# Differential attention heads: the inverse slope goes into q, the score correction products use 128 rows with zeros, and the DMA scratch is 8 KB

## The chip, the cores and the metric

The kernel runs on one core of one Trainium2 chip. The metric is the time of one execution on the device in microseconds (us), as the median of several runs. Five engines work side by side, each through its own list of instructions in order: TensorE (PE; its weight loads are shown as PEld), VectorE (DVE), ScalarE (ACT), GpSimd (POOL) and SyncE (SP), which issues most of the loads from memory. POOL issues transfers too.

## The reference

The model is an encoder of two layers over 512 tokens of 1024 features. Each layer modulates its input, projects it, runs two kinds of attention side by side (eight heads with latent projections, "MLA", and eight differential heads), gates and adds their outputs, and adds the residual; then comes a feed-forward block (layer 0) or a mixture of eight experts with two per token (layer 1). What the change touches are the differential heads. Cut to that:

```python
slopes = 2.0 ** (-8.0 * jnp.arange(1, 9) / 8)          # 1/2, 1/4, ... 1/256
# q, k: [token, head, 2 halves, 64]; v: [token, head, 128]
sc = einsum('bqhmd,bkhmd->mbhqk', q, k) * 64 ** -0.5
sc = sc - slopes[h] * abs(pos_q - pos_k)
p = softmax(sc, axis=-1)
a = p[0] - lam * p[1]
o = einsum('bhqk,bkhd->bqhd', a, v)                    # then an RMS norm per head
```

A head has two halves of 64 features, each with scores and a softmax of its own; the slope of the distance halves from head to head.

## The kernel before, in words

All matrix products are made in a reduced float32 type (float32r). To keep float32 accuracy each operand is split into a larger part and a remainder, and three products are added: large by large, large by remainder and remainder by large (`mm3`, lines 127 to 129). For weights, `wsplit` does this: ACT copies the loaded tile to the larger part `wh` (L111), and DVE subtracts to get `wl` (L113). In the attention part this subtraction is done by POOL instead (`W["eng"] = G`), on tiles of 128x1024.

Layer by layer, `attention` first makes the latents of the MLA heads, and then runs a loop in which one head of each kind is worked on at a time, one's scores beside the other's values: for each head h, four MLA score units (a unit is 128 queries) beside the four value units of the differential head h, then four differential score units of head h+1 beside the four MLA value units. Products that are not yet needed (q, k and v of later heads, gates) are cut into steps and put in between by `plan` and `fill`, so that PE has work while a softmax is computed. `turned` (L444, L124) transposes 128 keys of the four units' probabilities on PE, so it needs the last of the four units: PE's step from a head's differential scores to its values is called a boundary below.

A differential score unit is `diff_score_unit`. q of a head is a tile of 128 rows by 2 by 512: for half m, the rows of that half hold the larger part and the other 64 rows the remainder; k holds its larger part twice. So one product of 128 rows (L726) makes both "large by large" and "remainder by large", and a correction product of 64 rows (L729) adds the larger part of q by k's remainder `dkl`. There are two of each per unit, one per half m, in two PSUM banks. Then DVE combines distances and scores and takes the row minimum (L734), ACT computes the exponentials and their sum (L736), DVE halves the distances of this unit in place for the next head (L739, not for the last head), takes the reciprocals (L740, L741), scales the second half's probabilities (L742) and subtracts them from the first's (L743). At the end of a pair of MLA heads DVE adds two halves of an output (L715) and POOL stores it in DRAM (L717). `diff_norm` squares and averages a head's output through PE (L765, L767) and stores it from POOL (L773); after the loop POOL loads all heads' outputs back (`ol`).

The code is written through a framework that plans each engine's order ahead of time from the dependences and estimated costs, so that an engine's instructions do not stand in exactly the order of the source; buffers that share memory are kept apart by waits that it adds. `order(a, b)` fixes the order of two instructions on one engine.

Of the kernel before, what the change touches and what calls it, by code (L numbers as in the profile page):

```python
# [10 lines left out]
F32 = mybir.dt.float32  # L11
# [8 lines left out]
S = 512  # L20
# [13 lines left out]
DIST0 = 0.5 / DIFF_SCALE      # the first head's slope over the scale  # L34
C_DQ, C_DK, C_DV, C_GA, C_GB = 672, 1696, 2720, 3744, 4768
PSB = (6, 2)
LAT = 416       # columns of the latents that are made first
SLOT = [336, 320, 128, 128, 64, 64, 64, 64]     # rows of each place, from the most used expert on
SLOT_ROWS = sum(SLOT)
N_OVER = 7      # most blocks of 128 rows that any routing can leave over  # L40
N_ROWS = SLOT_ROWS + N_OVER * P
HALVES = [(0, 512), (512, 512)]
PIECES = [(0, 512), (512, 256), (768, 256)]     # the experts' outputs, by columns, as they are combined
PACE = {336: 1.0, 320: 1.0, 128: 0.5, 64: 1.0}    # weight of a tile
# [12 lines left out]
def build(tc, I, out, dbg=None, upto=99):  # L57
# [5 lines left out]
    def nm(s):  # L63
        n_[0] += 1
        return f"{s}_{n_[0]}"
# [20 lines left out]
    def order(after, before):  # L86
        """keep two instructions of one engine in this order"""
        tc.add_manual_dep(after.ins, before.ins.name,
                          mybir.DependencyInfo(mybir.DependencyClass.NoSync, mybir.DependencyReason.DATA),
                          reason="order on one engine")  # L90
# [5 lines left out]
    behind = [None, 0]      # weights behind the next [1] are split after the Vector instruction [0]  # L96

# [55 lines left out]
    # columns of per-feature vectors: b_ada (48), q_norm_g (3), kv_norm_g (2), diff_norm_g (8)  # L153
# [33 lines left out]
    def columns_of(l, o, n, parts, dma):  # L187
        """rows of 128, transposed into columns o.. of cols[l]"""
        r = su.tile([n, P], F32, name=nm("rows"))
        i = 0  # L190
        for k in parts:
            v = I[k][l:l + 1].rearrange("o (k p) -> (o k) p", p=P)
            m = v.shape[0]
            dma(r[i:i + m], v)
            i += m
        pr = psum_t()
        T.transpose(pr[:, :n], r, ident[:n, :n])
        V.tensor_copy(cols[l][:, o:o + n], pr[:, :n])

    columns_of(0, 0, 48, ["b_ada"], A.dma_start)  # L200
# [1 line left out]
    def mod_steps(pool, todo, wait=2):  # L202
        """generator: a slice of the contraction at a time on the Vector engine; mods[l, v] holds the result:
        columns, one more than the value where it scales, or (one is None) the index of a row in DRAM"""
# [53 lines left out]
    def half_h(pool, xtiles, sc, sh, h, l, i):  # L258
        """half of the tokens (two tiles), into h and l"""
# [27 lines left out]
    def rstd_of(pool, var, eps, n):  # L287
        """(var + eps) ** -0.5 for [P, n]: a first guess from the bits, then Newton steps."""
# [18 lines left out]
    def ln_stat(pool, st, table):  # L307
# [3 lines left out]
        # (var + eps) ** -0.5: a guess from the tables, then a Newton step  # L311
# [8 lines left out]
    def fold(l, which, sc, sh):  # L320
        """scale and shift of the modulated LN output, from the normalised rows"""
# [8 lines left out]
    # ================= layers =================  # L330
# [7 lines left out]
    def first_h(k):  # L338
        """128 features of scale and shift, then of the first layer's input"""
# [8 lines left out]
        # four groups of columns share the contraction; their sums are added as they turn into columns  # L348
# [19 lines left out]
    def first_products(l, hTh, hTl, step):  # L368
        """half of the latents, and the first head's q and k, as the features of the input come"""
# [70 lines left out]
    def turned(pool, tiles, k):  # L440
        """one 128-key slice of the probabilities, transposed and split"""
# [8 lines left out]
    def attention(l, hTh, hTl, firsts, todo, before_mg=None, middle=None):  # L450
# [6 lines left out]
        # lambda  # L457
# [16 lines left out]
        # projections of the differential heads  # L474
        dp = st_o.enter_context(tc.tile_pool(name=nm("dp"), bufs=1))

        def proj_v(pair, ts):
            """values of two heads, token tiles ts, in steps"""
# [26 lines left out]
        def head_qk(h, which, pq):  # L505
            """a head's transposed -q or k, split: of q's two halves (m) the parts below each other, of k's
            the larger part twice, so that one product has q whole"""
            half = [slice(64 * m, 64 * m + 64) for m in range(2)]
            if which == 0:
                q = dp.tile([P, 2, S], F32R, name=nm("dq"), tag="dq", bufs=2)  # L510
                for m in range(2):
                    A.activation(q[half[m], m], pq[half[m]], AF.Copy, scale=-1.0)
                    V.scalar_tensor_tensor(q[half[1 - m], m], pq[half[m]], -1.0, q[half[m], m], op0=OP.mult, op1=OP.subtract)
                heads[h] = (q,)
            else:
                k = dp.tile([P, 2, S], F32R, name=nm("dk"), tag="dk", bufs=2)
                kl = dp.tile([P, S], F32R, name=nm("dkl"), tag="dkl", bufs=2)
                for m in range(2):
                    A.activation(k[half[m], m], pq[half[m]], AF.Copy)
                    V.tensor_tensor(kl[half[m]], pq[half[m]], k[half[m], m], op=OP.subtract)  # L520
# [9 lines left out]
        def proj_gate(m, i):  # L530
            """a gate's argument, for later"""
# [10 lines left out]
        def plan(*gens):  # L542
            """work that fills the tensor engine's time; its weights are loaded now"""
# [4 lines left out]
        def fill(n=None):  # L548
            """some steps of it, or all of it"""
# [6 lines left out]
        def rest():  # L556
            """what is still to be done, as a function"""
# [45 lines left out]
        # latents transposed, with the norm's gain  # L603
# [11 lines left out]
        # a head's values in two parts, side by side: the larger part is where the head's rows of oA are  # L615
        vv = mp.tile([P, NT, 8, 2, 64], F32R, name=nm("vv"), tag="vv")
        # rotary on the shared key part
# [11 lines left out]
        # queries: 3 groups of 256 columns  # L629
# [55 lines left out]
        def mla_score_unit(h, t):  # L685
# [5 lines left out]
            # e = -scale * scores, with its row minimum: minus the softmax's maximum  # L691
# [27 lines left out]
        def diff_score_unit(h, t):  # L719
# [7 lines left out]
            for m in range(2):  # L727
                rr = slice(64 * m, 64 * m + 64)
                last_mm[0] = T.matmul(scs[m], q[rr, m, tt], kl[rr], start=False, stop=True)  # L729
            for m in range(2):  # L730
                sc = scs[m]
                e = sm.tile([P, S], F32, name=nm("de"), tag="e", bufs=8)
                # minus the biased, scaled scores, and their row minimum
                V.tensor_tensor_reduce(e, dist[:, t, :], sc, scale=DIFF_SCALE, scalar=3.0e38,  # L734
# [3 lines left out]
            if h < 7:  # L738
                V.tensor_scalar(dist[:, t, :], dist[:, t, :], 0.5, None, op0=OP.mult)  # L739
# [37 lines left out]
        # a head of each kind at a time: one's scores beside the other's values, with projections in between  # L777
# [128 lines left out]
    def old_rows(pool, upool, xsrc, lnp):  # L906
        """the residual stream's token tiles, from DRAM; affine of the LN before, on GpSimd"""
# [13 lines left out]
    def residual(lhs, nk, w, per, stay, gi, xsrc, lnp, xdst, ab=None, upool=None, hook=None, early=None):  # L921
        """a block's output projection (lhs(k, t) @ w), residual and LN; the next transposed input."""
# [16 lines left out]
        for half in range(2):  # L939
# [4 lines left out]
            # the last tile by two halves, so that less is left behind the last product  # L944
# [57 lines left out]
    # the first products of what follows, over half of the tokens, then the other half  # L1002
# [49 lines left out]
    # feed-forward  # L1052
# [41 lines left out]
    FIRST = 2       # the place that starts: its tokens come from the chip, not from DRAM  # L1094
# [5 lines left out]
    def routing_constants():  # L1100
# [20 lines left out]
        # of each place: rows, first row, shift of the rows beyond them  # L1121
# [4 lines left out]
        # the router on the normalised rows: weights by the modulation's scale, bias by its shift  # L1126
# [15 lines left out]
    def route_tile(pool, us, t):  # L1142
        """the two experts of each token of a tile"""
# [41 lines left out]
    # ranks among the tokens of an expert, counts  # L1185
# [11 lines left out]
    # the order of the experts by count, the lower index first among equals  # L1197
    key = et([P, 8])
    V.scalar_tensor_tensor(key, cnt, 8.0, R["io8r"], op0=OP.mult, op1=OP.add)
    ahead = et(b88)     # [expert, expert ahead of it]  # L1200
# [3 lines left out]
    at = et(b88)        # [expert, place]  # L1204
# [7 lines left out]
    # each expert's rows, first row and shift of the rows beyond its place  # L1212
# [5 lines left out]
    # blocks beyond the places, and those of the experts ahead  # L1218
# [14 lines left out]
    # the row of each assignment  # L1233
# [22 lines left out]
    # gates  # L1256
# [8 lines left out]
    # number of the blocks beyond the places, and the expert of each  # L1265
# [6 lines left out]
    ge_s, lt_e = et(b88), et(b88)       # [block, expert]  # L1272
# [9 lines left out]
    # the first place's assignments as a matrix of ones  # L1282
# [16 lines left out]
    # tokens of the places' rows, 128 rows to a column; 64 for the small places  # L1299
# [9 lines left out]
    def modulated(columns, h, l_, o, n):  # L1309
        """n token columns (columns(pt, j) makes four of their feature tiles), modulated and split"""  # L1310
# [18 lines left out]
    def landed(xg, h, l_, o=0, n=P):  # L1329
        """n gathered rows, transposed, modulated and split into columns o.. of h and l_;  # L1330
        on the tensor engine behind the products traced so far, which can run before the rows arrive"""
# [9 lines left out]
    def picked(h, l_):  # L1341
        """the same for the place that starts: products with a matrix of ones"""
# [7 lines left out]
    def both(o, xs, wh, wl, start, stop):  # L1350
        """o = xs.T @ w for the 128 columns of xs: 64 tokens' larger parts, then their smaller ones.
        The product is the sum of o's two halves."""
# [396 lines left out]
```

## Time and profile before

| | us |
|---|---|
| median of 3 runs | 2599.07 |
| lowest and highest run | 2594.40 and 2599.55 |
| span of the profiled execution | 2593.2 |
| PE busy in it | 2448.9 (94%) |
| DVE busy | 1841.1 (71%) |
| ACT busy | 1438.8 (55%) |
| POOL busy | 409.3 (16%) |

The profile is of one execution, and what it gives of that execution's time is its span, from the first instruction to the last; the runs' times include what lies around the span. The attention loops take about 126 to 420 us in layer 0 and 1100 to 1380 us in layer 1; the experts run from about 1650 us to the end. An engine's time in a row is when it was occupied, not when it was useful: a locked or waiting instruction that has begun counts as busy. PE's products are pipelined, so the distance between two starts says more than a duration.

### The profile page before, as it was taken

The page shows a single profiled execution, that of the slowest core. Times are in us where ns is not written, and L with a number is a line of the kernel's source. Part 1 is how long each engine was busy: PE and PEld are TensorE (multiplying, and loading weights), DVE is VectorE, ACT ScalarE, POOL GpSimd, SP SyncE. Part 2 cuts the span into 40 slices and gives each one's busy share as a digit, 9 for nine tenths or more (in the row PEclk, how much of TensorE's full clock was granted, in tenths as well). Part 3 has the DMA queues.
Part 4 walks back from the last instruction along what each step waited for, and adds up shares of the span by engine and source line. Part 5 has one row for each costly group of instructions (what it writes and reads, how often), then busy time and mean ns, then how long its engine had stood idle before and what let it go on. Part 6 is the DMA issues. An engine that isn't in the chain of part 4 may idle for free.

```text
span 2593.2 us, 37066 instructions
## 1 busy us (share of the span) xinstructions
PE 2448.9 (94%) x13124; PEld 2077.7 (80%) x13124; DVE 1841.1 (71%) x2844; ACT 1438.8 (55%) x2320; POOL 409.3 (16%) x337
## 2 busy tenths in 40 slices
PE   8899999998999999999999997999999999999994
PEld 6877777787788888877777875788899998999994
DVE  3688886647665435688875346787788887988875
ACT  3677665223222214676765224766677778777761
POOL 1323231001000402323321032410000000000004
PEclk9999999999999999999999999999999999999997
DMA  8311225745866433212224326999899989999993
GB/s 231 90 57 58 70 66 166 229 154 187 284 220 198 149 98 108 74 58 78 58 68 157 98 98 194 321 328 300 291 318 292 329 290 308 336 301 332 291 342 120
DMA packets 453210, 502.20 MB, mean 194 GB/s; under 512 B 19314, under 2 KB 322920, under 8 KB 453016
## 3 DMA queue, kind: packets, MB, share of 16 engines
q1 hardware_dynamic: 437616, 453.64, 55.2%
q0 software_dynamic: 13888, 45.30, 5.0%
q8 instruction: 105, 1.72, 0.3%
q10 hardware_dynamic: 1512, 0.81, 0.1%
q14 instruction: 89, 0.73, 0.1%
HBM read 474.95 MB, written 24.74 MB: 193 GB/s over the span
## 4 chain that ended last, share of the span: by engine, by line
PE 72%; DVE 13%; DMA 6%; ACT 5%; issue 3%; POOL 2%; SPq 0%; ACTq 0%; POOLq 0%; DVEq 0%
PE ps L127 19%; PE ps L129 19%; PE ps L128 19%; PE ps L1353 5%; PE ps L1354 5%; PE pt L444 2%; DVE de L743 2%; DVE dist L739 1%; ACT de L736 1%; DVE wl L113 1%; DVE de L742 1%; DMA mst<-in_w_ada 1%; DMA ws<-in_ffn_w 1%; DMA ol<-o_dram 1%; DVE de L734 1%
## 5 line engine op out<-in xcount | busy, mean ns | idle before, releaser
L111 ACT ACTIVATE wh<-ws 128x1024 fp32r<-128x1024 f32 (+3 forms) x786 | 779.7, 1012 | 695.9 <-PE ps L128 343.4
L113 DVE TENSOR_TENSOR wl<-ws,wh 128x1024 fp32r<-128x1024 f32 (+3 forms) x712 | 840.8, 1200 | 351.1 <-ACT wh L111 345.1
L129 PE MATMUL ps<-hTh,wl 128*128 128x512 f32 (+1 forms) x904 | 352.0, 389 | 7.5 <-DVE wl L113 7.5
L127 PE MATMUL ps<-hTh,wh 128*128 128x512 f32 (+1 forms) x904 | 354.1, 392 | 0.1
L128 PE MATMUL ps<-hTl,wh 128*128 128x512 f32 (+1 forms) x904 | 349.8, 387 | 0.8 <-POOL hTl L282 0.8
L113 POOL TENSOR_TENSOR wl<-ws,wh 128x1024 fp32r<-128x1024 f32 (+1 forms) x74 | 179.5, 2427 | 268.7 <-ACT wh L111 180.2
L129 PE MATMUL ps<-x3h,wl 128*128 128x336 f32 (+1 forms) x704 | 220.3, 313 | 1.0 <-DVE wl L113 1.0
L127 PE MATMUL ps<-x3h,wh 128*128 128x336 f32 (+1 forms) x704 | 221.2, 314 | 0.0
L128 PE MATMUL ps<-x3l,wh 128*128 128x336 f32 (+1 forms) x704 | 219.9, 312 | 0.0
L129 PEld LDWEIGHTS ps<-hTh,wl 128*128 128x128 f32 x904 | 173.8, 192 | 41.3 <-DVE wl L113 8.4
L127 PEld LDWEIGHTS ps<-hTh,wh 128*128 128x128 f32 x904 | 172.5, 191 | 38.2 <-issue 7.7
L128 PEld LDWEIGHTS ps<-hTl,wh 128*128 128x128 f32 x904 | 172.7, 191 | 32.4 <-POOL hTl L282 2.0
L1353 PE MATMUL ps<-wh,xes 128*128 128x512 f32 (+1 forms) x384 | 143.3, 378 | 0.0
L1354 PE MATMUL ps<-wl,xes 128*128 128x512 f32 (+1 forms) x384 | 141.4, 374 | 0.0
L127 PEld LDWEIGHTS ps<-x3h,wh 128*128 128x128 f32 x704 | 132.4, 188 | 3.4
L128 PEld LDWEIGHTS ps<-x3l,wh 128*128 128x128 f32 x704 | 132.6, 188 | 3.0
L129 PEld LDWEIGHTS ps<-x3h,wl 128*128 128x128 f32 x704 | 132.1, 188 | 1.4 <-DVE wl L113 1.2
L127 PE MATMUL ps<-wh,hTh 128*128 128x256 f32 (+1 forms) x384 | 117.2, 307 | 1.4 <-ACT hTh L365 0.7
L124 DVE TENSOR_TENSOR pTl<-pt,pTh 128x512 fp32r<-128x512 f32 x128 | 86.7, 688 | 40.6 <-ACT pTh L123 38.8
L214 DVE SCALAR_TENSOR_TENSOR macc<-mst,condrep,macc 128x1024 f32<-128x1024 f32 x70 | 89.8, 1282 | 34.5 <-DMA mst<-in_w_ada 33.3
L128 PE MATMUL ps<-wl,hTh 128*128 128x256 f32 (+1 forms) x384 | 113.9, 298 | 0.0
L129 PE MATMUL ps<-wh,hTl 128*128 128x256 f32 (+1 forms) x384 | 113.3, 297 | 0.0
(425 smaller groups left out, 5364.6 us busy)
## 6 DMA issues: line engine op xcount, KB each, us to landing
ws<-in_moe_w SPq DMA_DIRECT2D x492, 512.0 KB, 5.9
ws<-in_w_in SPq DMA_DIRECT2D x94, 512.0 KB, 3.7
mst<-in_w_ada SPq DMA_DIRECT2D x80, 512.0 KB, 5.0
ws<-in_ffn_w SPq DMA_DIRECT2D x66, 512.0 KB, 4.0
ws<-in_moe_w SPq DMA_DIRECT2D x48, 256.0 KB, 3.7
wa<-in_w_ada SPq DMA_DIRECT2D x16, 512.0 KB, 6.6
ws<-in_w_br_diff SPq DMA_DIRECT2D x16, 512.0 KB, 3.6
ws<-in_w_out SPq DMA_DIRECT2D x16, 512.0 KB, 3.6
```

The source lines that it names most:

```text
L111: A.activation(h, st, AF.Copy)
L113: i = eng.tensor_tensor(l, st, h, op=OP.subtract)
L124: V.tensor_tensor(l, src, h, op=OP.subtract)
L127: T.matmul(o, ah, bh, start=start, stop=False)
L128: T.matmul(o, ah, bl, start=False, stop=False)
L129: last_mm[0] = T.matmul(o, al, bh, start=False, stop=stop)
L214: i = V.scalar_tensor_tensor(acc, st, condrep[:, k, 0:1], acc, op0=OP.mult, op1=OP.add)
L444: T.transpose(pt[:, t * P:(t + 1) * P], tiles[t][:, k * P:(k + 1) * P], ident)
L734: V.tensor_tensor_reduce(e, dist[:, t, :], sc, scale=DIFF_SCALE, scalar=3.0e38, op0=OP.add, op1=OP.min, accum_out=st[:, m:m + 1])
L743: V.scalar_tensor_tensor(ee[0], ee[0], st[:, 4:5], ee[1], op0=OP.mult, op1=OP.add)
L1353: T.matmul(o, xs, wh, start=start, stop=False)
L1354: T.matmul(o, xs, wl, start=False, stop=stop)
```

## The change

Four things change.

The distances are no longer halved: L739 goes. Instead q of head h is multiplied by -(2 to the h) where it was multiplied by -1, and the scale in L734 by 0.5 to the h, which gives the same biased scores.

The correction product of a half takes all 128 rows of q (`q[:, m, tt]`) where it took 64; `dkl` gets a second dimension for the halves, and the 64 rows that belong to the other half hold zeros. The zeros are written once per layer by POOL into two tiles that stay, one for even and one for odd heads (they were two rotating buffers of half the size).

The memory at the start of each partition that is set aside for the descriptors of transfers issued by POOL goes from 16 KB, the default, to 8 KB.

Comments are removed, which changes nothing that runs. The diff without them:

```diff
+        kls = [dp.tile([P, 2, S], F32R, name=nm("dkl"), tag=f"dkl{i}") for i in range(2)]
+        for kl in kls:
+            for m in range(2):
+                G.memset(kl[64 - 64 * m:128 - 64 * m, m].bitcast(F32), 0.0)
...
                 q = dp.tile([P, 2, S], F32R, name=nm("dq"), tag="dq", bufs=2)
+                up = -2.0 ** h
                 for m in range(2):
-                    A.activation(q[half[m], m], pq[half[m]], AF.Copy, scale=-1.0)
-                    V.scalar_tensor_tensor(q[half[1 - m], m], pq[half[m]], -1.0, q[half[m], m], op0=OP.mult, op1=OP.subtract)
+                    A.activation(q[half[m], m], pq[half[m]], AF.Copy, scale=up)
+                    V.scalar_tensor_tensor(q[half[1 - m], m], pq[half[m]], up, q[half[m], m], op0=OP.mult, op1=OP.subtract)
...
-                kl = dp.tile([P, S], F32R, name=nm("dkl"), tag="dkl", bufs=2)
+                kl = kls[h % 2]
                 for m in range(2):
                     A.activation(k[half[m], m], pq[half[m]], AF.Copy)
-                    V.tensor_tensor(kl[half[m]], pq[half[m]], k[half[m], m], op=OP.subtract)
+                    V.tensor_tensor(kl[half[m], m], pq[half[m]], k[half[m], m], op=OP.subtract)
...
             for m in range(2):
-                rr = slice(64 * m, 64 * m + 64)
-                last_mm[0] = T.matmul(scs[m], q[rr, m, tt], kl[rr], start=False, stop=True)
+                last_mm[0] = T.matmul(scs[m], q[:, m, tt], kl[:, m], start=False, stop=True)
...
-                V.tensor_tensor_reduce(e, dist[:, t, :], sc, scale=DIFF_SCALE, scalar=3.0e38,
+                V.tensor_tensor_reduce(e, dist[:, t, :], sc, scale=DIFF_SCALE * 0.5 ** h, scalar=3.0e38,
...
-            if h < 7:
-                V.tensor_scalar(dist[:, t, :], dist[:, t, :], 0.5, None, op0=OP.mult)
...
-    nc = bacc.Bacc("TRN2", target_bir_lowering=False, num_devices=1)
+    nc = bacc.Bacc("TRN2", target_bir_lowering=False, num_devices=1, dynamic_dma_scratch_size=8192)
```

## Rows read from the trace of the kernel before

**Rows 1.** The head of the page: the span and the number of instructions.

```profile
span 2593.2 us, 37066 instructions
```

**Rows 2.** Section 4 of the page, the chain of waits that ended last.

```profile
PE 72%; DVE 13%; DMA 6%; ACT 5%; issue 3%; POOL 2%; SPq 0%; ACTq 0%; POOLq 0%; DVEq 0%
```

**Rows 3.** Stretches: us, busy PE, PEld, DVE, ACT, POOL (instructions), clock, DMA share, GB/s.

```profile
0.00:120.00 120.00, 104.65 (x718) 88.23 (x718) 61.07 (x167) 55.66 (x119) 32.18 (x54) 0.99 0.59 166
126.00:376.00 250.00, 229.79 (x1218) 180.44 (x1216) 212.17 (x465) 179.08 (x361) 75.53 (x41) 0.98 0.22 63
```

**Rows 4.** PE's waits, 120 to 1376 us: total us, times, the longest.

```profile
PE pt L444 <- DVE de L743: 39.0, 14, 3.4
```

**Rows 5.** Instructions of the line L739: ns min/median/max, first and last start.

```profile
L739 DVE TENSOR_SCALAR dist<-dist x56: 407/427/2628, 129.9 to 1332.6; 128x512 f32<-128x512 f32 x56
```

**Rows 6.** Timeline of PE, two score units: start, us, engine, line, operation, tiles, shapes.

```profile
200.28 0.71 PE L726 MATMUL ps<-dk,dq 128*128 128x512 f32 x2
200.92 0.50 PE L729 MATMUL ps<-dkl,dq 64*128 64x512 f32 x2
201.36 0.50 PE L127 MATMUL ps<-hTh,wh 128*128 128x512 f32 x1
201.69 0.40 PE L128 MATMUL ps<-hTl,wh 128*128 128x512 f32 x1
201.93 0.39 PE L129 MATMUL ps<-hTh,wl 128*128 128x512 f32 x1
...
205.26 0.63 PE L726 MATMUL ps<-dk,dq 128*128 128x512 f32 x2
...
206.59 0.39 PE L767 MATMUL ps<-osql,mean 128*128 128x512 f32 x1
```

**Rows 7.** Timeline of all engines at a boundary of the first kind.

```profile
181.17 2.40 POOL L113 TENSOR_TENSOR wl<-ws,wh 128x1024 fp32r<-128x1024 f32 x1 [5.19 <-issue]
...
181.41 2.44 DVE L739 TENSOR_SCALAR dist<-dist 128x512 f32<-128x512 f32 x1
...
182.26 0.19 ACT L736 ACTIVATION_READ_ACCUMULATOR de<-de,dst 128x1 f32 x1
...
183.78 0.15 DVE L740 RECIPROCAL dst<-dst 128x2 f32<-128x2 f32 x1
...
185.62 0.57 POOL L717 DMA_DIRECT2D o_dram<-o  x1 [2.04 <-DVE o L715]
...
186.20 2.35 POOL L113 TENSOR_TENSOR wl<-ws,wh 128x1024 fp32r<-128x1024 f32 x1
186.21 2.90 DVE L743 SCALAR_TENSOR_TENSOR de<-de,dst,de 128x512 f32<-128x512 f32 x1
```

**Rows 8.** Timeline of all engines at a boundary of the second kind.

```profile
219.78 2.63 DVE L739 TENSOR_SCALAR dist<-dist 128x512 f32<-128x512 f32 x1
...
220.81 0.19 ACT L736 ACTIVATION_READ_ACCUMULATOR de<-de,dst 128x1 f32 x1
...
223.05 2.37 POOL L113 TENSOR_TENSOR wl<-ws,wh 128x1024 fp32r<-128x1024 f32 x1 [0.93 <-ACT wh L111]
...
223.67 2.03 DVE L742 TENSOR_SCALAR de<-de,dst 128x512 f32<-128x512 f32 x1
...
225.96 0.73 DVE L743 SCALAR_TENSOR_TENSOR de<-de,dst,de 128x512 f32<-128x512 f32 x1
```

**Rows 9.** Busy time and granted clock (PEclk) behind three boundaries, columns as above.

```profile
188.60:192.00 3.40, 2.83 (x8) 2.35 (x9) 1.87 (x4) 1.69 (x3) 0.00 (x0) 0.50 0.58 154
226.10:229.50 3.40, 2.75 (x12) 2.04 (x13) 2.13 (x5) 1.69 (x3) 0.00 (x0) 1.00 0.58 159
1188.70:1192.10 3.40, 3.40 (x10) 2.66 (x9) 1.55 (x3) 1.19 (x3) 0.00 (x0) 0.50 0.37 109
```

**Rows 10.** The one large memset before, line L1057: ns min/median/max.

```profile
L1057 POOL MEMSET zero<- x1: 932/932/932, 621.4 to 621.4; 128x512 f32 x1
```

**Rows 11.** DMA: the largest issues of POOL's queue: KB each, median us to landing.

```profile
ol<-o_dram POOLq DMA_DIRECT2D x4, 1024.0 KB, 8.3
```

More of the change, by code (lines that the diff above doesn't have):

```diff
@@ L726, in diff_score_unit @@
                 T.matmul(scs[m], q[:, m, tt], k[:, m], start=True, stop=False)
-            for m in range(2):
-                rr = slice(64 * m, 64 * m + 64)
-                last_mm[0] = T.matmul(scs[m], q[rr, m, tt], kl[rr], start=False, stop=True)
+                last_mm[0] = T.matmul(scs[m], q[:, m, tt], kl[:, m], start=False, stop=True)
             for m in range(2):
```

## The prediction, on record before the result

> **What bounds the kernel now.** I read the head of the page, the chain of waits by engine, and then busy time by stretch. The span is 2593.2 us [rows 1]. The chain is 72% PE and 13% DVE, so a DVE instruction matters only where it stands in that chain [rows 2]. Everything the diff touches runs in the two attention loops, about 126 to 376 us and its like in layer 1. In the first of them PE is busy 229.8 of 250 us, DVE 212.2, POOL 75.5, DMA 0.22 [rows 3]: no load bounds it, and neither PE nor DVE is saturated. So I asked what PE waits for there: 14 waits, 39.0 us in total, each for L743, the last step of the fourth score unit before PE may transpose the probabilities [rows 4]. Two layers with eight heads have seven such boundaries each. Elsewhere in the loop PE starts a product of 512 columns every 0.23 to 0.24 us [rows 6].
>
> Next, why L743 is late. L739 takes 0.43 us in the median but up to 2.63 [rows 5]; L743 takes 2.90 at one boundary and 0.73 at the next [rows 7, 8]. The timelines of two neighbouring boundaries explain it: at 181.41 L739 starts 0.24 us after a weight split of POOL (2.40 us) and ends with it; at 186.21 L743 comes just behind the next split (186.20) and again lasts until that is over [rows 7]. In the other kind, L739 waits for the split before (219.78, 2.63 us) and L742 for the next (2.03 us), and L743 goes free [rows 8]. The two kinds alternate. Of the 14 boundaries, the first of each layer is of neither kind, six are like [rows 7] (PE waits 3.45 us) and six like [rows 8] (2.47 us); 6 x 3.45 + 6 x 2.47 = 35.5 leaves 3.5 of the 39.0 us for the two first ones.
>
> **The change part by part.**
>
> *Halving removed, 56 instructions.* Most of them (median 0.43 us) fall where DVE soon waits for the exponentials of ACT anyway, so I give them nothing beyond the boundaries. At a boundary of the first kind the step behind, L740, needs the second exponential, whose sum is read until 182.26+0.19 = 182.45; it ran at 183.78. Without L739 it can run 183.78-182.45 = 1.3 us earlier, and so can L715, L742 and the value tile's L124 behind it in DVE's order. What is late next is POOL's second split: it stands in POOL's queue behind the transfer of L715's output (185.62, released by L715, 0.57 us) and starts at 186.20, at the moment at which DVE comes to L743 (186.21) [rows 7]. Both hang on L715, so both move by 1.3 us, and L743 loses again. Gain 1.3 us, six times: 7.8 us. Bounds: 0 (another wait fills it) to 3.45 us (L743 ahead of the split, no wait left).
>
> At a boundary of the second kind DVE may go on at 220.81+0.19 = 221.00, where L739 held it to 219.78+2.63 = 222.41 [rows 8]. L715 and L742 follow some 1.3 us earlier, L742 at about 222.4 for 223.67, but the split at 223.05 is released by ACT's weight copy and stays. L742 ends ahead of the split, the split then takes its place, and L743 waits for all of it, to 223.05+2.37 = 225.4 or a little over, and needs 0.73: it ends at 226.2 to 226.3 where it ended at 226.7. Gain 0.4 us, six times: 2.4 us. Bounds 0 to 2.47.
>
> At the first boundary of a layer L739 stands ahead of a step that waits for ACT: 0. At the last there is none.
>
> *Correction products of 128 rows.* Before, the two 64-row products of a unit run at the same time: the two together take 0.50 us, as long as the single product behind them [rows 6]. Taken alone, that would make two full passes dearer. But the row also shows what surrounds the pair. From the first score product at 200.28 to the second of the products behind the pair at 201.69 are 1.41 us for what after the change is five full passes; the pass there takes 201.93-201.69 = 0.24, elsewhere 0.23. Five at 0.23 are 1.16: a gain of 0.25 us. In the next unit 205.26 to 206.59 are 1.33 us: a gain of 0.17. Sum 0.42 for the two units of a head that lie in the stretch in which PE is on the path, about 189 to 207 us; the other two of a head lie beside the DVE and ACT chain and only make PE wait longer. Sixteen heads: 6.7 us. Bounds: the slowest step of one pass in these rows is 0.33 (201.36 to 201.69); five such passes are 1.65 against 1.41, a loss of 0.24 a unit and 8 us over 32 units. On the other side all 64 units count: 64 x 0.21 = 13 us. I take the value between, since 0.23 to 0.24 is the step wherever the shape doesn't change.
>
> The Trainium skill speaks against this edit: "TensorEngine Tiling (Array Packing)", section Theoretical Speedup, gives products of at most 64 rows up to twice the throughput, so that giving it up would cost one pass of 0.23 us per unit, 32 x 0.23 = 7.4 us on the path by [rows 6]. The same page, section Key Properties, says that a change of the tiling mode drains the engine, and the trace's 0.33 us steps before and behind the pair fit that; by this the sum is the gain above.
>
> *Zeros.* Eight memsets of 64x512 on POOL, four per layer, once. The nearest row is a 128x512 memset of 0.93 us [rows 10]; at that price 3.7 us per layer. POOL is busy 32.2 of the first 120 us [rows 3], so I take 0: its idle time there hides them. Uncovered, ahead of a weight split for which PE waits, they would cost 7.4 us in both layers.
>
> *Half the DMA scratch, and q's scale.* The scale is another constant in instructions that stay: 0. The scratch serves the transfers that POOL issues, the largest of them 1024 KB with 8.3 us to landing [rows 11]. I take 0; the price if POOL has to wait is a rival below.
>
> *Clock.* Behind a wait of the first kind the granted clock is 0.50 (1.2 GHz) for 3.4 us, PE being busy 2.83 of them: at 2.4 GHz the same work takes 1.4 us less. After a wait of the second kind it is 1.00 in five cases (226.1 is one), and 0.50 once, at 1188.7 [rows 9]. The first kind shrinks from 3.45 to 3.45-1.3+0.4 = 2.55 us (0.4 from the units off the path), the size of the second, so five of six such stretches should go: 5 x 1.4 = 7.0 us.
>
> Sum: 7.8+2.4+6.7+7.0 = 23.9 us off the profiled span, 2593.2 to 2569.3. The profile gives the span alone; the median of the runs, 2599.07, is 5.8 us longer and the fastest run 1.2. I take the sum from the median: 2575.
>
> **The rivals.**
>
> *L743 wins the race.* With L715's transfer earlier or L124 placed ahead of L742, L743 starts before the split and PE does not wait. Only in the first kind: 6 x 3.45 + 2.4 + 6.7 + 8.4 (six clock stretches) = 38, 2561 us. In both, with all units on the path and the seventh clock stretch: 35.5 + 13 + 9.8 = 58, 2541. For: the two start 0.01 us apart [rows 7]. Against: both hang on the same step, and the order was the same at each of the six.
>
> *The wait fills up again.* What DVE gains is taken by the next locked step and the slow clock stays: only PE's 6.7 us, 2592. For: L742 and L743 already take turns in waiting [rows 7, 8]. Against: L740 would have been ready 1.3 us before.
>
> *Slower: POOL waits for its scratch.* If half the scratch holds less than what is in flight, a transfer of POOL waits until one before has landed. The place is the reload of the heads' outputs behind each attention, three issues in a row: two of them would be issued 8.3 us later each, less what they already wait in the queues, say 8 us a layer as an estimate, and as much again, 16 us by the same estimate, at POOL's gathers at the end. 16+16-24 = +8: 2607. It decides from the point where one 1024 KB issue needs more than half the scratch. For: these issues are the largest. Against: POOL's own queue has 0% of the chain [rows 2]. The Trainium skill, "DMA: Bandwidth & Descriptors", section Terms, gives 16 bytes for a descriptor; by that 8192 bytes are 512 places, and 1024 KB in pieces of 2 KB spread over 16 DMA engines need some 32 (an estimate from that page): it would not decide here, and no run shows it.
>
> *The order is planned anew* and L743 goes behind more work: that belongs to the second rival, at worst at no change.
>
> **How the numbers follow.** Forecast as worked out (2565 to 2586): 0.52. Race won: 0.18. Filled up: 0.18. Slower: 0.12. A measurement of this kernel can tell about 0.2%, 5.2 us, from no change. Faster by more: 0.52+0.18 and half of the 0.18, 0.79; within: the other half and 0.01 of the last, 0.10; slower 0.11. The range runs from between the two prices of the won race to just inside no change, 2547 to 2597.
>
> **What would show it.** No L739; L742 and L743 alternate as before, with L743 now blocked for 2.3 us and more at all twelve boundaries; PE's 14 waits for L743 sum to about 6 x 2.55 + 6 x 2.47 + 3.5 = 34 us instead of 39.0; four products of a unit at 0.23 us steps; half clock in one or two places per layer. The forecast is wrong if PE's waits vanish (first rival), stay at 39 us (second), or if POOL's issues lie farther apart than now (third).

## The result, and the profile after

The changed kernel takes 2560.36 us (median of 4 runs, 2555.66 to 2565.49), the kernel before 2597.53 beside it: a ratio of 0.985, with a 95% interval of 0.9834 to 0.9865. That is 37 us less, where 24 were forecast. The profiled execution took 2559.58 us, its span is 2557.8 [rows 1: 2593.2].

Lines moved by 2 to 6: the score products L726 and L729 are now L732 and L733, the exponentials L736 are L740, the reciprocals L740 and L741 are L742 and L743, the scaling L742 is L744, and the subtraction for which PE waits, L743, is **L745**; the sum of an output's halves, L715, is L721, and its store, L717, is L723. L739 is gone. The line in which PE waits for it, 120 to 1376 us, answers to [rows 4]:

```profile
PE pt L444 <- DVE de L745: 19.3, 8, 2.7
```

So 39.0 us in 14 waits became 19.3 in 8. Six boundaries have no wait any more. The timeline of a boundary of the first kind [rows 7] shows who is left:

```profile
181.69 2.41 POOL L113 TENSOR_TENSOR wl<-ws,wh 128x1024 fp32r<-128x1024 f32 x1 [4.87 <-issue]
...
183.19 0.17 DVE L742 RECIPROCAL dst<-dst 128x2 f32<-128x2 f32 x1 [0.98 <-ACT de L740]
183.28 0.67 DVE L698 TENSOR_SCALAR_CACHE_REDUCE e<-ps 128x512 f32<-128x512 f32 x1
...
183.87 0.24 DVE L743 TENSOR_TENSOR dst<-dst,nlam 128x1 f32<-128x1 f32 x1
...
185.13 0.57 POOL L723 DMA_DIRECT2D o_dram<-o  x1 [1.03 <-DVE o L721]
...
185.72 2.36 POOL L113 TENSOR_TENSOR wl<-ws,wh 128x1024 fp32r<-128x1024 f32 x1
185.73 2.91 DVE L745 SCALAR_TENSOR_TENSOR de<-de,dst,de 128x512 f32<-128x512 f32 x1
```

The second split still comes 0.01 us ahead of the subtraction, which then takes 2.91 us. What stands beside the first split also tells which steps of DVE are held up: L698 reads from PSUM and runs at its usual 0.67 us, while L743, 128x1 with both operands in SBUF (0.16 us elsewhere), lasts to the split's end (183.87+0.24 = 184.11 against 181.69+2.41 = 184.10). A boundary of the second kind [rows 8]:

```profile
219.69 0.22 DVE L743 TENSOR_TENSOR dst<-dst,nlam 128x1 f32<-128x1 f32 x1
219.84 0.67 DVE L721 TENSOR_TENSOR o<-o,ps 64x512 f32<-64x512 f32 x1
...
220.43 0.47 DVE L744 TENSOR_SCALAR de<-de,dst 128x512 f32<-128x512 f32 x1
220.83 0.41 DVE L124 TENSOR_TENSOR dv<-ps,dv 128x256 fp32r<-128x256 f32 x1
...
221.03 3.12 POOL L113 TENSOR_TENSOR wl<-ws,wh 128x1024 fp32r<-128x1024 f32 x1 [1.14 <-ACT wh L111]
221.16 0.73 DVE L745 SCALAR_TENSOR_TENSOR de<-de,dst,de 128x512 f32<-128x512 f32 x1
```

Here the split is the one that waits: 3.12 us instead of 2.4, longer by L745's 0.73. DVE has come to the subtraction in time. PE's score unit, as in [rows 6]:

```profile
203.55 0.40 PE L732 MATMUL ps<-dk,dq 128*128 128x512 f32 x1
203.79 0.40 PE L733 MATMUL ps<-dkl,dq 128*128 128x512 f32 x1
204.02 0.40 PE L732 MATMUL ps<-dk,dq 128*128 128x512 f32 x1
204.26 0.39 PE L733 MATMUL ps<-dkl,dq 128*128 128x512 f32 x1
204.48 0.40 PE L767 MATMUL ps<-osqh,mean 128*128 128x512 f32 x1
204.72 0.39 PE L769 MATMUL ps<-osql,mean 128*128 128x512 f32 x1
```

Four products in steps of 0.23 us; from the first to the second one behind them 204.72-203.55 = 1.17 us, before 1.33 and 1.41. Over the 62 units of each kernel whose products stand together in the trace the mean is 1.14, before 1.30: 0.16 us a unit. (The change also makes one loop over the halves of two, which the diff in the section on the change leaves out; a half's two products then stand together. The prediction did not see that. It is tried below.)

The stretch in layer 0 and the clock behind three boundaries (first, second, first kind), columns as in [rows 3, 9]:

```profile
126.00:376.00 250.00, 239.59 (x1296) 197.51 (x1296) 195.30 (x464) 191.58 (x384) 80.96 (x43) 0.99 0.24 67
188.60:192.00 3.40, 3.31 (x17) 2.53 (x18) 2.06 (x6) 1.70 (x3) 0.00 (x0) 1.00 0.59 154
222.00:225.40 3.40, 3.40 (x18) 2.62 (x18) 1.95 (x4) 1.70 (x3) 2.15 (x1) 1.00 0.35 113
258.90:262.30 3.40, 3.40 (x10) 2.56 (x10) 1.99 (x4) 0.60 (x2) 0.00 (x0) 0.52 0.46 135
```

Within the attention loops of both layers, and the few us ahead of their first score product, half clock (1.2 GHz) stands in 4 stretches of 3.4 us, before in 8, in one profiled execution each. At 1.4 us each [rows 9] that is 5.6 us; where PE is busy for all of the 3.40 us, as from 258.9 on, the same sum gives 1.7 each.

**Where the 37 us come from.** From the second head's first score product to the last product of `diff_norm`, layer 0's loop went from 255.2 to 238.2 us and layer 1's from 256.8 to 239.3: 34.5 of the span's 35.4. These stretches leave out the first boundary of each layer, at which PE waited 1.8 us before and 2.24 after. What is left of the waits is 39.0-3.6 = 35.4 before and 19.3-4.5 = 14.8 after, 20.6 less; 56 units x 0.16 = 9.0 are the products'; half clock fell from 7 stretches in them to 3, 5.6 us. Together 35.2 for 34.5: the account closes to within 1 us, with half clock as its least certain term.

### The profile page after: what moved, and what is told of

The parts are those of the page before. It is cut to its first block, busy times and chain, and to the rows that moved or that the text cites. A ratio compares the mean times of both kernels' runs of the same rounds, so it can differ in the third digit from the quotient of the medians.

```text
span 2557.8 us, 37042 instructions
## 1 busy us (share of the span) xinstructions
PE 2434.5 (95%) x13124; PEld 2087.2 (82%) x13124; DVE 1789.0 (70%) x2788; ACT 1441.7 (56%) x2320; POOL 418.6 (16%) x345
## 4 chain that ended last, share of the span: by engine, by line
PE 75%; DVE 9%; DMA 6%; ACT 5%; issue 3%; POOL 1%; SPq 0%; ACTq 0%; DVEq 0%; POOLq 0%
PE ps L127 20%; PE ps L128 20%; PE ps L129 19%; PE ps L1355 5%; PE ps L1356 5%; PE pt L444 2%; DVE de L745 1%; DMA ws<-in_moe_w 1%; DVE wl L113 1%; DMA mst<-in_w_ada 1%; ACT de L740 1%; ACT wh L111 1%; PE ps L732 1%; PE ps L733 1%; DMA ws<-in_ffn_w 1%
```

## The experiments

Theory at the start: the gain is a race between POOL's weight split and DVE's subtraction, which the earlier DVE chain wins at one kind of boundary; the products and the clock add the rest. Rivals: the parts simply add; or the time of DVE's own work counts; or the order of the products or the scratch does something.

### The parts alone

**Halving alone removed** (`e1`): the scale moves into q, L739 goes, 64-row products and 16 KB stay.

```diff
-                    A.activation(q[half[m], m], pq[half[m]], AF.Copy, scale=-1.0)
+                    A.activation(q[half[m], m], pq[half[m]], AF.Copy, scale=up)
...
-            if h < 7:
-                V.tensor_scalar(dist[:, t, :], dist[:, t, :], 0.5, None, op0=OP.mult)
```

> Only the halving goes (q takes the inverse slope); products of 64 rows, old scratch. Theory (L739 held L743 back at the boundaries, and that is the larger part): PE's waits for L743 fall from 39.0 us to about 22, half clock in the loops in four places for eight, time about 2597-17-5 = 2575. Rival (PE's products are the larger part): waits stay above 33 us, time 2588 or more.

Measured: 2583.44 us, 0.994 (0.9921 to 0.9959), some 15 us less: between the theory's 2575 and the rival's 2588. PE's waits sum to 28.4 us in 14, where about 22 were expected: 2.44 at the first kind, 1.75 at the second; half clock stands in 6 places, where 4 were. The second kind, DVE and POOL:

```profile
220.52 0.41 DVE L740 TENSOR_TENSOR dst<-dst,nlam 128x1 f32<-128x1 f32 x1
220.86 0.67 DVE L716 TENSOR_TENSOR o<-o,ps 64x512 f32<-64x512 f32 x1
221.45 0.47 DVE L741 TENSOR_SCALAR de<-de,dst 128x512 f32<-128x512 f32 x1
221.84 2.37 POOL L113 TENSOR_TENSOR wl<-ws,wh 128x1024 fp32r<-128x1024 f32 x1 [0.93 <-ACT wh L111]
221.85 0.41 DVE L124 TENSOR_TENSOR dv<-ps,dv 128x256 fp32r<-128x256 f32 x1
222.18 2.58 DVE L742 SCALAR_TENSOR_TENSOR de<-de,dst,de 128x512 f32<-128x512 f32 x1
```

This is what the prediction described: the scaling (here L741) ahead of the split, the split next, and the subtraction (here L742) behind it. With this part alone the race is lost at both kinds.

**128-row products alone** (`e2`: `kls`, the zeros and 8 KB scratch; the halving and the old order of the products stay).

```diff
-                last_mm[0] = T.matmul(scs[m], q[rr, m, tt], kl[rr], start=False, stop=True)
+                last_mm[0] = T.matmul(scs[m], q[:, m, tt], kl[:, m], start=False, stop=True)
```

> Only the 128-row correction products with zeros (with the 8 KB scratch that makes room); distances are still halved, and the four products of a unit stand in the order of before. Theory: a unit becomes 0.16 us shorter on PE, which counts for two of a head's four units, the other two make PE wait longer: waits for L743 39 to 44 us, time 2597-5 = 2592 (2587 to 2597). Rival (PE's products are the larger part): 2575 to 2582, waits not longer.

Measured: 2599.01 us, 0.9998 (0.9984 to 1.0011): no gain, and above the expected 2587 to 2597. The units are 0.14 us shorter here too, which is 9 us. But PE's waits are 40.3 us in 14, and in the profiled execution more of it runs at half clock. Three of these stretches, columns as above:

```profile
159.60:163.00 3.40, 3.40 (x10) 2.33 (x9) 1.99 (x4) 0.82 (x2) 0.00 (x0) 0.50 0.03 9
197.20:200.60 3.40, 3.40 (x10) 2.40 (x9) 1.99 (x4) 0.75 (x2) 0.00 (x0) 0.50 0.44 131
234.70:238.10 3.40, 3.40 (x10) 2.44 (x9) 1.99 (x4) 0.71 (x2) 0.00 (x0) 0.50 0.23 67
```

They come once per head, some 37.5 us apart; counted in 3.4 us there are 16 where there were 8, 8 x 1.4 = 11 us given back. How far that holds for the medians is not shown. Over whole executions the mean granted clock is 0.974 in this one and 0.979 in the profiled one of the kernel before, but the medians are 0.975 over e2's 12 runs and 0.976 over the 27 of the kernel before beside them, which alone go from 0.974 to 0.982. So e1 and e2 give 15 and 0, and together 37: the parts do not add.

**Scratch alone** (`e3`) and **the old order of the products** in the kernel after (`e6`):

```diff
-    nc = bacc.Bacc("TRN2", target_bir_lowering=False, num_devices=1)
+    nc = bacc.Bacc("TRN2", target_bir_lowering=False, num_devices=1, dynamic_dma_scratch_size=8192)
```

> Only the DMA scratch of 8 KB. Theory: no difference, within 5 us of before, POOL's issues as far apart as before. Rival 1 (POOL waits for room): slower by 8 us or more. Rival 2 (the other places of the buffers free some wait outside the loops, where some 3.6 us of the gain lie): 3 to 4 us faster, in the stretch ahead of layer 1's loop.

```diff
             for m in range(2):
                 T.matmul(scs[m], q[:, m, tt], k[:, m], start=True, stop=False)
+            for m in range(2):
                 last_mm[0] = T.matmul(scs[m], q[:, m, tt], kl[:, m], start=False, stop=True)
```

> The kernel after, but the four products of a unit in the order of before (both halves' first products, then both corrections), where the change puts a half's two together. Theory (the order plays no part): as after, 2560 +- 3, no waits at boundaries of the second kind. Rival (a half's scores that are ready one product earlier let DVE come in time to L743 at the second kind): there PE waits 2 us or more again, time 2560+6 x 2.4 = 2574.

Measured: 2600.0 us for the scratch, 1.0008 (0.9994 to 1.0023); 2559.54 for the order, 0.9853 (0.9829 to 0.9877), with 18.8 us of waits in 8. Neither does anything.

### The race moved

**Halving kept, but behind the subtraction** (`e4`, the kernel before with `order` on the halving of each unit).

> The kernel before with all its halvings, but each behind the unit's last step L743 on DVE instead of ahead of L740. Theory (not DVE's work counts but the lock in which the halving stood ahead of the exponentials' use): PE's waits per boundary as with the halving removed alone, 2.4 and 1.8 us for 3.4 and 2.5, time 2583 +- 4. Rival (DVE's load counts): as before, 2598.

Measured: 2595.66 us, 0.9979 (0.9966 to 0.9992): 4 us less, where 15 were expected. The waits fell to 26.7 us, below those of e1 with no halving at all: for the waits, what counts is the halving's place ahead of the reciprocals, not the 0.43 us that it takes of DVE. Why 12 us of waits gave 4 us of time is shown in part only. In the profiled execution half clock stands in 12 stretches instead of 8, with waits of 1.93 us at every boundary for 3.43 and 2.47 in turns; but over all runs the mean granted clock is 0.977 in the median, for e4 as for the kernel before.

**The value tile's remainder behind the subtraction** (`e5` on the kernel after, `e7` on e1; `e8` is e5 with k's remainder behind it too).

```diff
-                split(v0[:, t, :], v1[:, t, :], pv[:, :256])
+                A.activation(v0[:, t, :], pv[:, :256], AF.Copy)
+                i = V.tensor_tensor(v1[:, t, :], pv[:, :256], v0[:, t, :], op=OP.subtract)
+                if last_diff[0] is not None:
+                    order(i, last_diff[0])
```

> The kernel after, with one more order on DVE: a value tile's remainder (0.41 us) comes behind the last score unit's subtraction and not ahead of it. Theory (a race with POOL's second weight split decides the wait): the subtraction comes 0.4 us earlier, ahead of the split, at the first kind too; PE's six waits of 2.4 us go, 2560-6 x 2.4 = 2545. Rival (the split is not what it waits for): 2560.

> Only the halving removed, products of 64 rows and the old scratch, with the same order on DVE (the value tile behind the subtraction). Theory (what the two edits do together beyond their sum is the race, which the shorter products win at the second kind): with the order the race is won without them, waits at both kinds go, 2583-6 x 2.4-6 x 1.75 = 2558, some 10 us of products above the kernel after with that order. Rival (the 128-row products give the rest by themselves): 2575 to 2583.

> As the kernel after with the value tile behind the subtraction, and the remainder of k behind it too, which stands ahead of it at the first boundary of a layer. Theory: the two waits of 2.2 us there go as well, 2545-4 = 2541. Rival: k's remainder is late next, and PE waits for the products that need it: not faster than the order of the value tile alone.

Measured: e5 2565.98 us, 0.9869 (0.9853 to 0.9885); e7 2599.49, 1.0002 (0.999 to 1.0014); e8 2567.96, 0.9882 (0.9865 to 0.9898). All three miss: slower than without the order, by 6, 16 and 8 us (in e8 the waits at the first boundaries stay at 2.24 us). A boundary of the first kind of e5, where the subtraction is L749, says why:

```profile
185.48 0.48 DVE L748 TENSOR_SCALAR de<-de,dst 128x512 f32<-128x512 f32 x1
185.75 0.57 POOL L727 DMA_DIRECT2D o_dram<-o  x1 [1.04 <-DVE o L725]
186.00 3.24 DVE L749 SCALAR_TENSOR_TENSOR de<-de,dst,de 128x512 f32<-128x512 f32 x1
186.34 2.34 POOL L113 TENSOR_TENSOR wl<-ws,wh 128x1024 fp32r<-128x1024 f32 x1
```

L749 starts 0.34 us ahead of the split and is held all the same: POOL is issuing its transfer at that time, and the split follows it by 0.02 us. It is so at all six boundaries of this kind, in e7 and e8 too. At the second kind, where no issue stands ahead of the split, 0.10 us are enough in e5:

```profile
223.15 0.75 DVE L749 SCALAR_TENSOR_TENSOR de<-de,dst,de 128x512 f32<-128x512 f32 x1
223.25 2.91 POOL L113 TENSOR_TENSOR wl<-ws,wh 128x1024 fp32r<-128x1024 f32 x1 [1.14 <-ACT wh L111]
```

An issue alone holds nothing. In the kernel before the same operation, of the same shape and with both tensors in SBUF, begins 0.34 us into an issue with no split behind it and takes its usual time:

```profile
589.85 0.54 POOL L971 DMA_DIRECT2D xn_dram<-u  x1 [30.48 <-DVE u L970]
590.19 0.69 DVE L936 SCALAR_TENSOR_TENSOR u<-u,ftmp 128x512 f32<-128x512 f32 x1
```

So where a split follows directly on an issue, being 0.3 us ahead of the split is not enough; how the two together hold the subtraction is not shown. PE waits 2.88 us instead of 2.45, and half clock stands in 9 stretches in e5 (4 in the kernel after), in 14 in e7 (6 in e1).

### The race won

**The output's sum behind the subtraction as well** (`e9` on e5, `e11` on e7). L721 releases the transfer, so with this both the issue and DVE's own detour go.

```diff
-                V.tensor_tensor(o[rr], o[rr], po[rr], op=OP.add)
+                i_o = V.tensor_tensor(o[rr], o[rr], po[rr], op=OP.add)
+                if last_diff[0] is not None:
+                    order(i_o, last_diff[0])
```

> The kernel after the change with two small steps of VectorE put behind the last subtraction of a unit (L745 in the kernel after): the sum of an MLA pair's two output halves (L721), and the remainder of the value tile (L124). Theory (whoever starts first keeps the two-input path; POOL's store of the sum, which is released by L721, also holds VectorE up): without L721 ahead of it L744 runs at 1.93 us behind the end of the last score step and L745 at 2.43, where POOL's second split comes at 3.0 and its store cannot come before; L745 then takes 0.73 us at all twelve boundaries, PE's wait of 2.45 us at the first kind is gone, and with it the half clock behind it: 6 x 2.45 + up to 4 x 1.4 = 15 to 20 us below the kernel after, 2540 to 2546. Rival (what has been put off is late next: L721 frees a PSUM bank and starts the store, L124 feeds the values): PE waits as long elsewhere, 2558 to 2568, as when L124 alone was put off.

> The kernel before with the halving alone removed (correction products of 64 rows) and the same two steps of VectorE behind the last subtraction. Theory: the race is decided by the place of the subtraction and not by the shorter products, so here too L743's like takes 0.73 us at all twelve boundaries and PE's waits of 2.44 and 1.75 us go: 25 us of waits and some half clock below that version's 2583, about 2550 to 2558, and above the same order with 128-row products by the products' own 10 us. Rival (only with the shorter products does VectorE come early enough): split and subtraction still lie within 0.2 us of each other, and the time stays at 2580 to 2600.

Measured: e9 2538.24 us, 0.9772 (0.9755 to 0.9789), a shade below the expected 2540 to 2546; e11 2551.15, 0.9819 (0.9803 to 0.9835), as expected. The subtraction in e9 (its L751; ns min/median/max):

```profile
L751 DVE SCALAR_TENSOR_TENSOR de<-de,dst,de x64: 736/743/755, 139.3 to 1314.4; 128x512 f32<-128x512 f32 x64
```

None of 64 is held up, in e11 neither (755 ns at most), and PE's waits for it are 3.4 us in e9 and 0.8 in e11. So the order of DVE alone decides the race, with either kind of products, and the products are worth 2551.15-2538.24 = 12.9 us where the race is no longer in play. In the profiled loops, counted as above and with no half clock in either, 469.8 us became 460.8: the 9.0 us are 56 units x 0.16, so here every unit counts.

### The lock taken away

**No split of POOL in the loops** (`e10` on the kernel after, `e12` on the kernel before; the edit also covers the latents ahead of a loop).

```diff
-        W["eng"] = G
+        W["eng"] = V
```

> The kernel after with the weights' remainders in the attention loops taken by VectorE too (128x1024 in 1.26 us, as elsewhere in the kernel) and none by POOL. Theory (VectorE's two-input steps are long only because POOL's split holds a path that both use): no step of VectorE in the loops lasts over 1.3 us, L745 never over 0.8; some 32 splits a layer put 40 us on VectorE, which is at 78% there, and less is blocked, so the time is about the same or up to 20 us longer, 2560 to 2580. Rival (L745 is long for another reason, such as a wait of its own): L745 is still 2.9 us at the first kind of boundary with no split of POOL beside it.

> The kernel before, unchanged but for the weights' remainders in the attention loops, which VectorE takes instead of POOL: what the change is worth where no split of POOL stands beside VectorE. Theory (of the change's 37 us some 20 are waits and 6 half clock, both from POOL's split, and 10 the products): L739, L742 and L743 never last beyond 0.8 us; PE's 39 us of waits for L743 shrink to under 10; the change is then worth the products' 10 us and what 56 halvings of 0.43 us cost an engine that is now fuller, and the time is 2538 to 2555, against 2528 for the same edit of the kernel after. Rival (the halving costs by its own 24 us of VectorE's time too): 2560 or more.

Measured: e10 2527.79 us, 0.9737 (0.9717 to 0.9757); e12 2542.99, 0.9788 (0.9774 to 0.9802), as expected. In e10 the subtraction, and its busy time in layer 0's stretch:

```profile
L745 DVE SCALAR_TENSOR_TENSOR de<-de,dst,de x64: 731/749/754, 129.3 to 1299.4; 128x512 f32<-128x512 f32 x64
```

```profile
126.00:376.00 250.00, 248.03 (x1343) 204.35 (x1342) 222.50 (x506) 192.88 (x391) 15.20 (x18) 1.00 0.26 71
```

In e12, the kernel before with nothing but this edit, the halving and the subtraction:

```profile
L739 DVE TENSOR_SCALAR dist<-dist x56: 409/420/430, 126.7 to 1287.1; 128x512 f32<-128x512 f32 x56
```

```profile
L743 DVE SCALAR_TENSOR_TENSOR de<-de,dst,de x64: 734/745/754, 130.0 to 1320.2; 128x512 f32<-128x512 f32 x64
```

L739 at most 0.43 us where it was 2.63 [rows 5], the subtraction at most 0.75 where it was 2.9: without POOL's split nothing holds these steps. PE's waits for the subtraction are 1.0 us in e12, and there is no half clock in the loops of either. The time was a miss in e10: same or slower was expected, since DVE gets 1.2 us for every split, and it became 33 us faster than the kernel after. DVE goes from 195.3 to 222.5 of the 250 us in that stretch and hides it. (That the weights come sooner from DVE, 1.2 us for 2.4, is no cause: in the account's stretches PE of the kernel before waits 35.4 us for L743 and 0.4 for all else.) The change is worth 2542.99-2527.79 = 15 us where POOL does not split, near the products' 10 to 13; the other 22 of its 37 us hang on POOL's split.

The Trainium skill, "SBUF — State Buffer", section "SBUF: two separate sides", describes one pair of ports between VectorE and GpSimd as "an exclusive lock, not a bandwidth split": whoever starts first keeps it for the whole instruction, for VectorE's two-port modes and, against a GpSimd step that reads SBUF, for its steps with two inputs in SBUF. The rows agree that one blocks the other: L745 2.91 us or the split 3.12, and neither when the other is away. They do not bear out "first" by the recorded starts: at the second kind of the kernel after the split is recorded 0.13 us ahead and L745 goes, and in e5 L749 is recorded ahead and the split goes.

## Why the prediction was right, and where it was not

The forecast of 2575 was on the right side, and 2560 lies in its range of 2547 to 2597; but it is 15 us off, and below the 2565 to 2586 of the forecast as worked out. That the first rival's price for one kind of boundary, 2561, is met is luck: there the race was won at the first kind, here at the second. On one footing (PE's waits; products over all 64 units; half clock in the loops):

| term | forecast | measured |
|---|---|---|
| waits, first kind, 6 | 6 x (3.45-2.55) = 5.4 | 6 x 0.95 = 5.7 |
| waits, second kind, 6 | 0 (2.47 stays) | 6 x 2.47 = 14.8 |
| waits, first of each layer | 0 | -0.9 |
| products | 64 x 0.21 = 13.4 (32 of them, 6.7, on the path) | 64 x 0.16 = 10.2 |
| half clock | 5 x 1.4 = 7.0 | 4 x 1.4 = 5.6 |

**First kind: right.** "Both hang on L715, so both move by 1.3 us, and L743 loses again" is what the rows show: split and subtraction 0.01 us apart as before, PE's wait 2.45 (2.69 once) where 2.55 was forecast.

**Second kind: wrong, and this is the step that failed:** "L742 ends ahead of the split, the split then takes its place, and L743 waits for all of it." With the halving alone it is so (e1: 2.58 us, wait 1.75, so 0.7 us gained for the 0.4 forecast). In the whole change it is not, because the parts act on each other: the shorter score products let PE release the weight buffer earlier, so that POOL's first split ends, by the starts in the traces, 1.87 us behind the unit's last score step instead of 2.2 in e1. L743, which that split holds, then takes 0.22 us instead of 0.41, and DVE comes to the subtraction 0.35 us earlier (3.14 us behind that score step instead of 3.48, at the boundaries shown). The second split comes only 0.13 earlier (3.01 instead of 3.14). That the products make the difference is shown by e1 and the kernel after, since neither the scratch (e3) nor the order (e6) does; the zeros were not tried apart. The forecast let the first split stand where it was when it priced the products. The rival "L743 wins the race" allowed for the first kind alone or both; the second kind alone was no case of it.

**Products: right in size, wrong in where they count.** 0.16 us a unit against 0.17 to 0.25; but all units are on the path, not two of four: the account needs them, and e11 and e9 show it where no waits are left. The loss of 7.4 us that the prediction worked out by the Trainium skill, "TensorEngine Tiling (Array Packing)", section Theoretical Speedup, did not come: the runs have four full passes shorter than two and a pair. The gain is not safe by itself: in e2 nothing of it is left.

**Clock: the size about right, the reason too simple.** Four stretches fewer, five forecast. But the wait's length is not what rules it: 2.45 us or a little more leave half clock at three of six boundaries of the first kind here, 1.93 us go with 12 stretches in e4, and e2, with the waits of before, has 16 for 8. These are counts of one execution each, and the granted clock differs between executions of one kernel (0.974 to 0.982 in the kernel before), so the term is the least certain of the table.

**Zeros, scratch, scale: 0, as forecast.** e3 shows the scratch; `ol` lands in 8.0 us [rows 11: 8.3], so the slower rival had no ground. The zeros were tried only within e2, whose time is that of before; the four memsets of layer 0 take 2.1 us of POOL (3.7 were priced).

**The signs.** "L743 now blocked for 2.3 us and more at all twelve boundaries" and 34 us of waits were wrong (six, and 19.3); 0.23 us steps and one or two places of half clock per layer were right.

**Open.** Where split and subtraction come within about 0.13 us of each other the records do not tell who goes first: 0.13 us ahead by the profile, the split loses in the kernel after, and 0.12 ahead it wins in e7:

```profile
224.14 2.36 POOL L113 TENSOR_TENSOR wl<-ws,wh 128x1024 fp32r<-128x1024 f32 x1 [0.92 <-ACT wh L111]
224.26 2.79 DVE L746 SCALAR_TENSOR_TENSOR de<-de,dst,de 128x512 f32<-128x512 f32 x1
```

Why half clock stands at some boundaries and not at others with the same wait is open too; that it goes with the waits is shown by e10 and e12. So is why e4 gained no more than 4 us. And e10 is 10 us faster than e9 though its loops are no shorter (231.9 and 230.3 us in layer 0, counted as above): in layer 0 alone its first differential score product comes 9.8 us earlier (119.6 and 129.4). The same lock accounts for most of that: ahead of the loop POOL's splits hold DVE in e9 (L301, 128x8, takes 1.83 us beside one, 0.17 in e10), PE waits 3.1 us for L611, and half clock stands for 10.2 us; e10 has neither. That is 3.1+3 x 1.4 = 7.3 us.

## What to carry to other kernels

When a short VectorE step on SBUF operands shows a maximum several times its median, look for the GpSimd instruction that ends with it: removing such steps pays only if the next one wins the race, and taking GpSimd's part away (56 us on the kernel before) can be worth more than the edits that shift the race (46 in e11). Price the edits of a change together where a race decides, for 0.35 us on another engine's release turned 0.7 us per boundary into 2.5. Test an order of instructions by what it releases on the other engine, not only by whom it puts first.

## What was not expected of the hardware

With a transfer's issue (0.57 us) directly ahead of it, POOL's split held a two-operand step of VectorE that had begun 0.34 us earlier (e5, 3.24 us for a step of 0.74), while an issue alone held none (0.69 us at 590.19 in the kernel before). A shorter PE stream can be worth nothing by itself: e2's units are 0.14 us shorter, half clock went from 8 to 16 stretches in the profiled executions, and the time stayed at 2599.01.
